# Two MLPs of a decoder trunk on one core: sweeps that begin with three plain pairs, chunks turned by half banks, and first conversions two pairs ahead

## The chip, the cores and the metric

The kernel runs on 1 core of one Trainium2 chip. The metric is the time of one execution on the device in microseconds (us), as the median of several runs. TensorE (PE in the profile, PEld for its weight loads) multiplies, ScalarE (ACT) and VectorE (DVE) convert, evacuate and normalise, SyncE (SP) issues the loads. All weights stream from HBM once.

## The reference

A trunk of two layers on 256 tokens of width 2048, in float32. Layer 0 mixes tokens by retention, layer 1 by block-sparse attention. Each layer then has an MLP and a gated per-layer embedding; every step begins with an RMS norm of the residual stream `h`.

```
def sq_relu_mlp(xn, w_up, w_down):
    return jnp.square(jax.nn.relu(xn @ w_up)) @ w_down

def per_layer_embed(h, p_i, g, w_up, w_gate):
    gate = jax.nn.sigmoid(rms_norm(h, g) @ w_gate)
    return (p_i @ w_up) * gate

for i in range(DEPTH):
    h = h + (retention or moba_attention)(rms_norm(h, ...))
    h = h + sq_relu_mlp(rms_norm(h, mlp_norm_g[i]), mlp_w_up[i], mlp_w_down[i])
    h = h + per_layer_embed(h, p[i], ple_norm_g[i], ple_w_up[i], ple_w_gate[i])
```

w_up is 2048 x 8192, w_down 8192 x 2048. The change concerns the product with w_down and what follows it.

## The kernel before

**High and low halves.** TensorE works on float32r. Every operand is split into a rounded high half and the remainder: `split` has ACT cast the high half and DVE subtract it from the source. A product is three matmuls (high by high, high by low, low by high). Weights arrive in raw pairs of 128 x 2048 float32, 1 MB, in `RAWS = 3` buffers; a load is issued on SP when an earlier raw buffer is free. The halves go to `wh` and `wl`, rings of `RING = 3` buffers each.

**Units.** The program is a list of units, each a run of matmuls on TensorE (as a rule on half a raw pair). Beside it stand two kinds of work with a due unit: conversions in the list `prep`, written ahead of the unit they are due at, and tasks (`at`), written behind theirs. `run` writes it all out in this order, and each engine executes its own instructions in the order written, so that an instruction that waits holds up all behind it on its engine.

**The MLP.** In `mlp` each layer goes through two halves of the 8192 columns. `phase_a` makes the activations of a half in 32 up tiles of 128 (two units each, names `up`). Each tile occupies one of four PSUM banks (tag `mm`) until `fold` has emptied it: ACT copies one half of the bank (L254), DVE adds the other (L255). Then DVE clamps and scales (L650), ACT squares (L651), and `split` makes the operand `a`. After that come two sweeps per half, so four per layer (sweeps 1 to 4; `dn00`, `dn01`, `dn10`, `dn11` in the program, `dn_` with a number in the trace). A sweep adds the product of all activations of the half with 1024 columns of w_down to two chunks of `h`, each 512 wide, for both groups t of 128 tokens.

**Plain and fast pairs.** A sweep (`sweep`) has 16 raw pairs of two units. A plain pair has 8 products, 4 per unit, into the four banks C00, C01, C10, C11 (first digit t, second the chunk): 24 matmuls. The pairs in `FAST` use a Strassen-like scheme with 7 products, 21 matmuls: 9 in the first unit, 12 in the second. For it DVE forms sums of the raw weights (`sums`, L605 to L607, `tsum`), `corner` converts three quarters of the raw pair for the first unit, and the sums are converted for the second (`wide`), which starts with the product into bank P5. `due` says ahead of which unit a pair's conversions are written: the first unit of the ring buffer before.

**The end of a sweep.** Behind the last fast pair, `rest` adds up the fast products in four tasks (`one` to `four`, L685 to L699), one after each of the next units. `done` adds the C banks to `h` on DVE (L672), for t = 0 behind the last unit but one, for t = 1 behind the last. The banks so emptied are those that the next sweep, or the embedding, takes. In the second half the sweep has then finished two chunks of `h`, and `finish` prepares them as operands of the next norm: `square` on ACT, then `turn`, eight transposes on TensorE into two banks (tag `aux`, two in all), and `split`, which calls `scaled` four times: each time ACT (L261) and then DVE (L262) reads half a bank, ACT and DVE taking turns. Sweep 4 is followed by the embedding (`ple`): four units `pu` of 12 matmuls into two banks of the tag `mm` each, which ACT copies out (L736), then the gate's units, which need the turned chunks.

Of the kernel before, what the change touches and what calls it, by code (L numbers as in the profile page):

```python
# [10 lines left out]
F32 = mybir.dt.float32  # L11
F32R = mybir.dt.float32r
I32 = mybir.dt.int32
AF = mybir.ActivationFunctionType
ALU = mybir.AluOpType
AX = mybir.AxisListType

P = 128
S = 256
# [18 lines left out]
WARM = 9  # L38
FILL = 5
BR = 32  # L40
FAST = (2, 4, 6, 9, 11, 13)
RAWS = 3
RING = 3
G_RET, G_MLP0, G_PLE0, G_KV, G_ATT, G_MLP1, G_PLE1, G_FIN = range(8)
# [36 lines left out]
class Core:  # L81
# [175 lines left out]
    def scaled(self, n, g, src):  # L257
# [4 lines left out]
        self.nc.vector.scalar_tensor_tensor(t[:, S:], src, gs, t[:, :S].bitcast(F32), op0=ALU.mult, op1=ALU.subtract)  # L262
        return t

    def square(self, c):

        if c == 0:
            self.ssq = self.cp.tile([P, 2, KD // 4], F32, name="ssq", tag="ssq", bufs=2)
        for t in range(2):
            self.nc.scalar.activation(self.slot("sq"), self.h[c][:, t], AF.Square, accum_out=self.ssq[:, t, c:c + 1])  # L270

    def finish(self, c, i, gains):

        self.square(c)
        st = {}

        def turn():
            for a in range(2):
                ps = st[a] = self.aux("xt")
                for b in range(2):  # L280
                    for t in range(2):
                        o, f = 2 * b + t, 2 * a + b
                        self.nc.tensor.transpose(ps[:, o * P:(o + 1) * P], self.h[c][:, t, f * P:(f + 1) * P], self.ident)

        def split(f, g, xs):
            n, b = 4 * c + f, f % 2
            xs[n] = self.scaled(n, g, st[f // 2][:, b * S:(b + 1) * S])
        self.at(i + 1, turn)
        for f in range(4):
            self.at(i + 1 + f // 2, lambda f=f: split(f, gains[0], self.xx))  # L290
            if len(gains) > 1:
                self.at(i + 3 + f, lambda f=f: split(f, gains[1], self.x2))
# [256 lines left out]
    def sweep(self, name, src, first, pairs, x, done, rest):  # L549

        banks, left = {}, {}
        tags = {"P1": "y", "P5": "y", "Q6": "aux", "Q7": "aux"}

        def add(s, ops):
            for bank, _, _ in ops:
                left[bank] = left.get(bank, 0) + 1

            def mm():
                h, l = (s[n].rearrange("p a (b c) -> p (a b) c", b=2) for n in "hl")
                m = self.nc.tensor.matmul  # L560
                for bank, which, j in ops:
                    start = bank not in banks
                    if start:
                        banks[bank] = self.bank(f"{name}{bank}_", *((tags[bank], 2) if bank in tags else ()))
                    left[bank] -= 1
                    ps, (xh, xl) = banks[bank], x(*which)
                    m(ps, xh, h[:, j], start=start, stop=False)
                    m(ps, xh, l[:, j], start=False, stop=False)
                    m(ps, xl, h[:, j], start=False, stop=left[bank] == 0)
            self.units.append(mm)  # L570
            return len(self.units) - 1
        for q in range(pairs):
            a, b, due = 2 * q, 2 * q + 1, self.slots[-1]["first"]
            s = self.begin(src, first + q)
            if q in FAST:
                last = q
                add(s, [("C01", (q, "S4"), 1), ("C00", (b, 0), 2), ("P1", (a, 0), 0)])
                t = {"first": len(self.units), "pair": s["pair"]}
                self.slots.append(t)
                e = add(t, [("P5", (q, "S1"), 0), ("Q6", (q, "S2"), 1), ("C10", (b, 1), 2), ("Q7", (q, "S3"), 3)])  # L580
                self.prep.append((due, lambda s=s, t=t: self.sums(s, t)))
                self.prep.append((due, lambda s=s: self.corner(s)))
                self.prep.append((s["first"], lambda t=t: self.wide(t, t["t"], 2 * UC)))
            else:
                for r in range(2):
                    i = add(s, [(f"C{r}{c}", (k, r), j) for c, ks in ((0, ((a, 0), (b, 2))), (1, ((a, 3), (b, 1)))) for k, j in ks])
                self.prep.append((due, lambda s=s: self.whole(s)))
        for n, fn in enumerate(rest(banks)):
            self.at(e + 1 + n, fn)
        self.at(i - 1, lambda: done(banks, 0, i))  # L590
        self.at(i, lambda: done(banks, 1, i))
# [17 lines left out]
    def mlp(self, layer, gains):  # L609
        nc = self.nc  # L610
        v = nc.vector
        st = {}
        b = len(self.units)
# [8 lines left out]
        def x(k, t):  # L622
# [5 lines left out]
            z = act[k]  # L628
            if k // 2 in FAST and k % 2 == 0:
                return z[:, 0], z[:, 1]  # L630
            return z[:, t * P:(t + 1) * P], z[:, S + t * P:S + (t + 1) * P]

        def combine(q):
            z = pair.pop(q).rearrange("p a (b c) -> p (a b) c", b=2)
            f = self.slot("sf", (P, 4, P))
            v.tensor_sub(f[:, 0:2], z[:, 0::3], z[:, 1:2].to_broadcast([P, 2, P]))
            v.tensor_add(f[:, 2], f[:, 1], z[:, 0])
            v.tensor_sub(f[:, 3], z[:, 2], f[:, 2])
            sums[q] = h, l = self.slot("sh", dt=F32R), self.slot("sl", dt=F32R)
            self.split(h, l, f.rearrange("p a b -> p (a b)"))  # L640
        for half in range(2):
            def evac_up(n, ps, half=half):
                q = n // 2
                if n % 2 == 0:
                    pair[q] = self.slot("t", (P, 2, S))
                t = pair[q][:, n % 2]
                self.fold(t, ps)
                for _ in range(4 if half == 0 and n < LEAD else 1):
                    yield
                v.scalar_tensor_tensor(t, t, 0.0, st["rb"], op0=ALU.max, op1=ALU.mult)  # L650
                nc.scalar.activation(t, t, AF.Square)  # L651
                if q in FAST and n % 2 == 0:
                    j = FAST.index(q)
                    if j % 2 == 0:
                        st["c"] = self.slot("ac", (P, 4, P), F32R)
                    act[n] = st["c"][:, 2 * (j % 2):2 * (j % 2) + 2]
                    self.split(act[n][:, 0], act[n][:, 1], t[:, :P])
                else:
                    act[n] = self.slot(f"a{n}", dt=F32R)
                    self.split(act[n][:, :S], act[n][:, S:], t)  # L660
                if n % 2:
                    if q not in FAST:
                        pair.pop(q)
                        return
                    yield
                    combine(q)
            self.phase_a(f"up{half}_", f"mlp_up{layer}", half * 64, 32, 2, 1 if half else LEAD, lambda k: self.xx[k], evac_up)

            def done(banks, t, i, g, half=half):
                for c in range(2):  # L670
                    h = self.h[2 * g + c][:, t]
                    v.tensor_add(h, h, banks[f"C{t}{c}"])  # L672
                if half and t:
                    for c in range(2):
                        self.finish(2 * g + c, i + 2 * c, gains)

            def rest(banks, g):
                z = {}

                def h(t, c):  # L680
                    return self.h[2 * g + c][:, t]

                def one():
                    z["q"], z["u"] = self.slot("q"), self.slot("u")
                    nc.scalar.copy(z["q"], banks["P1"])  # L685
                    v.tensor_add(h(0, 0), h(0, 0), z["q"])

                def two():
                    v.tensor_sub(z["q"], z["q"], banks["Q6"])
                    v.tensor_add(z["u"], z["q"], banks["P5"])  # L690
                    v.tensor_sub(h(0, 1), h(0, 1), z["u"])

                def three():
                    v.tensor_add(z["q"], z["q"], banks["Q7"])
                    v.tensor_add(h(1, 0), h(1, 0), z["q"])

                def four():
                    v.tensor_add(z["q"], z["q"], banks["P5"])
                    v.tensor_sub(h(1, 1), h(1, 1), z["q"])  # L699
                return [one, two, three, four]  # L700

            src, n = f"mlp_dn{layer}", FH // 256
            for g in range(2):
                self.sweep(f"dn{half}{g}_", src, (half * 2 + g) * n, n, x, lambda banks, t, i, g=g, done=done: done(banks, t, i, g),
                           lambda banks, g=g, rest=rest: rest(banks, g))
# [357 lines left out]
```

## Time and profile before

| | us |
|---|---|
| median of 3 runs (lowest, highest) | 2752.36 (2751.19, 2755.58) |
| the profiled execution, its own time | 2752.92 |
| its span, from the first instruction to the last | 2750.5 |
| TensorE busy, share of the span | 2722.4, 99% |
| DVE busy, ACT busy | 1924.7, 1406.5 |

The profile is of one execution. Its time is 2.42 us more than its span, and 0.56 us more than the median. Sweep 1 of layer 0 starts at 925.80 us of the span, sweep 2 at 1010.60, sweep 3 at 1271.69, sweep 4 at 1355.07 and the embedding behind it at 1446.75; in layer 1 sweep 1 starts at 2115.97, sweep 3 at 2462.09, sweep 4 at 2545.47, the embedding at 2637.25. In rows of the timeline the first number is the start in us and the second the time taken; brackets tell how long the engine was idle before it, and what released it. The granted clock is TensorE's, 1.00 being full speed.

### The profile page before, as it was taken

The numbers are of one execution on the slowest core, as the hardware profiler recorded it, in microseconds if no ns is written. First come the engines' busy times: TensorE is split into PE (matmuls) and PEld (weight loads), VectorE is DVE, ScalarE is ACT, GpSimd is POOL, SyncE is SP. The second block draws the span as 40 slices with busy tenths as digits, with TensorE's granted clock in tenths as the row PEclk, the third lists the DMA queues.
The fourth block names the chain that finished last, engine by engine and source line by source line (L and its number), as shares of the span: only waits on it lengthen the run. The fifth ranks groups of instructions, "written<-read, shape, count | busy, mean of one in ns | idle before, by whom it ended". The sixth has DMA issues, their size and how long they took to land.

```text
span 2750.5 us, 33950 instructions
## 1 busy us (share of the span) xinstructions
PE 2722.4 (99%) x13608; PEld 2310.3 (84%) x13608; DVE 1924.7 (70%) x2543; ACT 1406.5 (51%) x1926; POOL 0.2 (0%) x4
## 2 busy tenths in 40 slices
PE   9999999999999999999999999999999999999998
PEld 8888888888888888888787888888888888888786
DVE  7766666655566788667786677675676887668775
ACT  6444444444455545555555655554555445554554
POOL 0000000000000000000000000000000000000000
PEclk9999999999999999999999999999999999999999
DMA  7555555445555555555554555555455655545453
GB/s 285 185 187 186 187 187 181 180 181 199 183 178 199 188 199 214 184 199 184 184 211 176 180 188 176 176 184 184 168 200 179 215 191 198 197 175 213 171 209 138
DMA packets 79449, 522.48 MB, mean 190 GB/s; under 512 B 8987, under 2 KB 12988, under 8 KB 17596
## 3 DMA queue, kind: packets, MB, share of 16 engines
q1 hardware_dynamic: 78476, 519.20, 52.7%
q10 hardware_dynamic: 816, 1.11, 0.3%
q8 instruction: 107, 1.75, 0.3%
q14 instruction: 50, 0.41, 0.0%
HBM read 517.39 MB, written 2.88 MB: 189 GB/s over the span
## 4 chain that ended last, share of the span: by engine, by line
PE 81%; DVE 10%; ACT 7%; issue 2%; DMA 0%; ACTq 0%; SPq 0%; DVEq 0%
PE up L183 9%; DVE wl L250 6%; PE up L181 5%; ACT wh L249 4%; PE qk L183 4%; PE aq L183 2%; PE ak L183 2%; PE qk L181 2%; PE aq L181 1%; PE ak L181 1%; ACT t L651 1%; DVE t L650 1%; ACT a L249 1%; DVE t L255 1%; PE y L492 1%
## 5 line engine op out<-in xcount | busy, mean ns | idle before, releaser
L250 DVE TENSOR_TENSOR wl<-raw,wh 128x1024 fp32r<-128x1024 f32 (+3 forms) x843 | 1121.5, 1350 | 396.3 <-ACT wh L249 396.0
L249 ACT CAST wh<-raw 128x1024 fp32r<-128x1024 f32 (+3 forms) x843 | 952.3, 1151 | 370.3 <-issue 77.9
L183 PE MATMUL up<-x,wh 128*128 128x512 f32 x2048 | 490.5, 391 | 0.0
L183 PEld LDWEIGHTS up<-x,wh 128*128 128x128 f32 x2048 | 376.0, 188 | 72.5
L181 PEld LDWEIGHTS up<-x,wl 128*128 128x128 f32 x2048 | 263.3, 191 | 10.9 <-issue 0.6
L181 PE MATMUL up<-x,wl 128*128 128x256 f32 x2048 | 267.0, 283 | 0.0
L249 ACT CAST wh<-tsum 128x2048 fp32r<-128x2048 f32 x48 | 91.8, 1913 | 161.0 <-DVE tsum L607 129.0
L651 ACT ACTIVATE t<-t 128x256 f32<-128x256 f32 x128 | 53.5, 418 | 228.5 <-DVE t L650 228.5
L250 DVE TENSOR_TENSOR wl<-tsum,wh 128x2048 fp32r<-128x2048 f32 x48 | 110.0, 2292 | 29.1 <-ACT wh L249 29.1
L250 DVE TENSOR_TENSOR a<-t,a 128x256 fp32r<-128x256 f32 x104 | 44.3, 426 | 95.9 <-ACT a L249 95.9
L183 PE MATMUL qk<-x,wh 128*128 128x512 f32 x448 | 109.9, 392 | 0.0
L183 PEld LDWEIGHTS qk<-x,wh 128*128 128x128 f32 x448 | 81.8, 188 | 15.5
L261 ACT ACTIVATE x<-xt,g 128x256 fp32r<-128x256 f32 x112 | 52.1, 478 | 52.6 <-DVE x L262 43.4
L262 DVE SCALAR_TENSOR_TENSOR x<-xt,g,x 128x256 fp32r<-128x256 f32 x112 | 52.7, 482 | 27.4 <-ACT x L261 26.2
L254 ACT COPY t<-up 128x256 f32<-128x256 f32 x128 | 47.0, 367 | 44.9 <-PE up L183 44.8
L183 PE MATMUL aq<-x,wh 128*128 128x512 f32 x256 | 63.3, 391 | 0.0
L183 PE MATMUL ak<-x,wh 128*128 128x512 f32 x256 | 62.9, 391 | 0.0
L270 ACT ACTIVATE sq<-h 128x512 f32<-128x512 f32 x48 | 30.1, 627 | 62.0 <-DVE h L534 27.7
L181 PEld LDWEIGHTS qk<-x,wl 128*128 128x128 f32 x448 | 57.4, 191 | 2.2
L255 DVE TENSOR_TENSOR t<-t,up 128x256 f32<-128x256 f32 x128 | 53.2, 416 | 7.7 <-ACT t L254 7.4
L605 DVE TENSOR_TENSOR tsum<-raw 128x1024 f32<-128x1024 f32 x48 | 58.5, 1218 | 0.0
L181 PE MATMUL qk<-x,wl 128*128 128x256 f32 x448 | 58.1, 283 | 0.0
(1191 smaller groups left out, 5301.2 us busy)
## 6 DMA issues: line engine op xcount, KB each, us to landing
raw<-mlp_up SPq DMA_DIRECT2D x128, 1024.0 KB, 4.8
raw<-mlp_dn SPq DMA_DIRECT2D x128, 1024.0 KB, 4.8
raw<-ret_in SPq DMA_DIRECT2D x94, 1024.0 KB, 4.8
raw<-att SPq DMA_DIRECT2D x48, 1024.0 KB, 4.8
raw<-ret_out SPq DMA_DIRECT2D x32, 1024.0 KB, 4.8
raw<-ple_gate SPq DMA_DIRECT2D x32, 1024.0 KB, 4.8
raw<-att_o SPq DMA_DIRECT2D x16, 1024.0 KB, 4.8
raw<-ple_up SPq DMA_DIRECT2D x4, 1024.0 KB, 5.0
```

Source lines behind the costliest of these rows:

```text
L181: mm(ps[:, S:], wl[:, c], rhs[k][:, :S], start=False, stop=end)
L183: mm(ps, wh[:, c], rhs[k], start=first and k == 0, stop=end)
L249: self.nc.scalar.copy(dst_h, src)
L250: self.nc.vector.tensor_sub(dst_l, src, dst_h.bitcast(F32))
L254: self.nc.scalar.copy(dst, ps[:, :S])
L255: self.nc.vector.tensor_add(dst, dst, ps[:, S:])
L261: self.nc.scalar.activation(t[:, :S], src, AF.Copy, scale=gs)
L262: self.nc.vector.scalar_tensor_tensor(t[:, S:], src, gs, t[:, :S].bitcast(F32), op0=ALU.mult, op1=ALU.subtract)
L270: self.nc.scalar.activation(self.slot("sq"), self.h[c][:, t], AF.Square, accum_out=self.ssq[:, t, c:c + 1])
L492: mm(ys[t], a, w, start=i == 0, stop=i == len(ops) - 1)
L605: v.tensor_add(o[:, 0::3], r[:, 0:2], r[:, 3:4].to_broadcast([P, 2, 512]))
L651: nc.scalar.activation(t, t, AF.Square)
```

## The change

It has three parts.

1. `FAST` begins at pair 3 and takes every other pair from there; as many pairs as before are fast.
2. `due` of the first two pairs of a sweep lies one ring buffer further ahead: pair 0's conversions are written ahead of the last but three unit of the stage before, pair 1's ahead of the last but one. Before, they were written ahead of the last but one and ahead of the sweep's own first unit.
3. Behind sweeps 3 and 4, `drip` takes the place of `finish`. It turns half a chunk at a time, four transposes into one bank, behind units 1, 2, 4 and 5 of sweep 4, or behind units 2, 3, 5 and 7 of the embedding, and one unit later `scaled2` makes two operands: ACT twice, then DVE twice. `finish` stays for the other stages.

```
-FAST = (2, 4, 6, 9, 11, 13)
+FAST = (3, 5, 7, 9, 11, 13)
...
+    def scaled2(self, n, g, src):
+        out = []
+        for b in range(2):
+            t = self.slot(f"x{g}_{n + b}", dt=F32R)
+            out.append((t, src[:, b * S:(b + 1) * S], self.g[:, g, n + b:n + b + 1]))
+        for t, x, gs in out:
+            self.nc.scalar.activation(t[:, :S], x, AF.Copy, scale=gs)
+        for t, x, gs in out:
+            self.nc.vector.scalar_tensor_tensor(t[:, S:], x, gs, t[:, :S].bitcast(F32), op0=ALU.mult, op1=ALU.subtract)
+        return [t for t, _, _ in out]
...
+    def turn(self, c, a):
+        ps = self.aux("xt")
+        for b in range(2):
+            for t in range(2):
+                o, f = 2 * b + t, 2 * a + b
+                self.nc.tensor.transpose(ps[:, o * P:(o + 1) * P], self.h[c][:, t, f * P:(f + 1) * P], self.ident)
+        return ps
+
+    def drip(self, c, when, gain):
+        self.square(c)
+        for a, i in enumerate(when):
+            def first(a=a, i=i):
+                ps = self.turn(c, a)
+
+                def second():
+                    n = 4 * c + 2 * a
+                    self.xx[n], self.xx[n + 1] = self.scaled2(n, gain, ps)
+                self.at(i + 1, second)
+            self.at(i, first)
...
-            a, b, due = 2 * q, 2 * q + 1, self.slots[-1]["first"]
+            a, b, due = 2 * q, 2 * q + 1, self.slots[-2 if q < FAST[0] - 1 else -1]["first"]
...
-                    for c in range(2):
-                        self.finish(2 * g + c, i + 2 * c, gains)
+                    for c, when in enumerate(((2, 3), (5, 7)) if g else ((1, 2), (4, 5))):
+                        self.drip(2 * g + c, [i + k for k in when], gains[0])
```

What DVE has in its queue between sweeps 1 and 2 of layer 0, from `one` (the first row) to the addition that empties C00 (the last). `wl_7933` is the low half of pair 0 of sweep 2. Before:

```order
L686 TENSOR_TENSOR h0_89<-h0_89,q_7913 128x512
L689 TENSOR_TENSOR q_7913<-q_7913,dn00_Q6__7529 128x512
L690 TENSOR_TENSOR u_7914<-q_7913,dn00_P5__7525 128x512
L691 TENSOR_TENSOR h1_90<-h1_90,u_7914 128x512
L250 TENSOR_TENSOR wl_7933<-raw_7838,wh_7932 128x2048
L694 TENSOR_TENSOR q_7913<-q_7913,dn00_Q7__7536 128x512
L695 TENSOR_TENSOR h0_89<-h0_89,q_7913 128x512
L672 TENSOR_TENSOR h0_89<-h0_89,dn00_C00__7438 128x512
```

The same piece of DVE's queue after, with `wl_7902` for pair 0 and `wl_7939` for pair 1:

```order
L250 TENSOR_TENSOR wl_7902<-raw_7838,wh_7901 128x2048
L715 TENSOR_TENSOR h0_89<-h0_89,q_7919 128x512
L718 TENSOR_TENSOR q_7919<-q_7919,dn00_Q6__7559 128x512
L719 TENSOR_TENSOR u_7920<-q_7919,dn00_P5__7555 128x512
L720 TENSOR_TENSOR h1_90<-h1_90,u_7920 128x512
L250 TENSOR_TENSOR wl_7939<-raw_7881,wh_7938 128x2048
L723 TENSOR_TENSOR q_7919<-q_7919,dn00_Q7__7566 128x512
L724 TENSOR_TENSOR h0_89<-h0_89,q_7919 128x512
L701 TENSOR_TENSOR h0_89<-h0_89,dn00_C00__7438 128x512
```

Pair 0's subtraction went ahead of `one`, and pair 1's, which had stood behind all four additions of C banks, came in ahead of `three`. The queue between sweeps 3 and 4 reads alike.

ACT's queue between the up tiles and sweep 1 of layer 0, from the copy of up tile 29 to the copy of tile 31. `wh_7386` is the high half of pair 0. Before:

```order
L254 COPY t_7286<-up0_29_7301 128x256
L651 ACTIVATE t_7286<-t_7286 128x256
L249 CAST a29_7364<-t_7286 128x256
L254 COPY t_7383<-up0_30_7345 128x256
L249 CAST wh_7386<-raw_7220 128x2048
L651 ACTIVATE t_7383<-t_7383 128x256
L249 CAST a30_7411<-t_7383 128x256
L254 COPY t_7383<-up0_31_7392 128x256
```

After, where `wh_7345` belongs to pair 0 and `wh_7392` to pair 1:

```order
L254 COPY t_7286<-up0_29_7301 128x256
L249 CAST wh_7345<-raw_7220 128x2048
L680 ACTIVATE t_7286<-t_7286 128x256
L249 CAST a29_7370<-t_7286 128x256
L254 COPY t_7389<-up0_30_7351 128x256
L249 CAST wh_7392<-raw_7268 128x2048
L680 ACTIVATE t_7389<-t_7389 128x256
L249 CAST a30_7417<-t_7389 128x256
L254 COPY t_7389<-up0_31_7398 128x256
```

One wide cast stood between the copies of tiles 29 and 31, now two do.

ACT's queue in the embedding behind sweep 4 of layer 0; `x2_8` to `x2_11` are operands made of the first turned chunk. Before:

```order
L736 COPY pu0_0_11254<-pu0_0_11247 128x512
L736 COPY pu0_1_11263<-pu0_1_11256 128x512
L261 ACTIVATE x2_8_11275<-xt_11265,g_72 128x256
L261 ACTIVATE x2_9_11278<-xt_11265,g_72 128x256
L249 CAST wh_11243<-raw_11154 128x1024
L736 COPY pu1_0_11292<-pu1_0_11285 128x512
L736 COPY pu1_1_11301<-pu1_1_11294 128x512
L261 ACTIVATE x2_10_11303<-xt_11270,g_72 128x256
```

After:

```order
L765 COPY pu0_0_11254<-pu0_0_11247 128x512
L765 COPY pu0_1_11263<-pu0_1_11256 128x512
L249 CAST wh_11243<-raw_11154 128x1024
L765 COPY pu1_0_11276<-pu1_0_11269 128x512
L765 COPY pu1_1_11285<-pu1_1_11278 128x512
L249 CAST wh_11292<-raw_11178 128x1024
L765 COPY pu2_0_11303<-pu2_0_11296 128x512
L765 COPY pu2_1_11312<-pu2_1_11305 128x512
L272 ACTIVATE x2_8_11319<-xt_11287,g_72 128x256
```

The operands of the turned chunk moved behind the copies of the units `pu1` and `pu2`.

More of the change, by code (lines that the diff above doesn't have):

```diff
@@ L278, in turn @@
             for a in range(2):
[L279 to L283, printed above, removed]
+                st[a] = self.turn(c, a)
         def split(f, g, xs):
```

## The prediction

> **What bounds the kernel now.** I read the page first, then the waits of TensorE, then counts of matmuls in stretches of equal length, then the timeline around each place where a count was low.
>
> ```profile
> span 2750.5 us, 33950 instructions
> PE 2722.4 (99%) x13608; PEld 2310.3 (84%) x13608; DVE 1924.7 (70%) x2543; ACT 1406.5 (51%) x1926; POOL 0.2 (0%) x4
> ```
>
> TensorE has work nearly all the time, and the change neither adds nor removes a matmul. So it can only win back what TensorE loses to waits, and only lose by making new ones. The waits (engine, line, who was waited for: total, times, longest):
>
> ```profile
> PE xt L283 <- DVE x L262: 4.5, 2, 2.3
> PE dn_P__10774 L567 <- ACT wh L249: 2.0, 1, 2.0
> ```
>
> All sizeable ones lie at starts of down-projection sweeps (`dn`) or just behind the last sweep of a layer (`xt`). A wait is priced too low there, since a matmul's end is modelled; so I count matmuls in stretches instead. Columns: stretch, length, busy time and count of PE, PEld, DVE, ACT, POOL, granted clock, DMA share, GB/s.
>
> ```profile
> 980.00:1010.00 30.00, 30.00 (x134) 24.86 (x133) 26.90 (x24) 15.38 (x9) 0.00 (x0) 1.00 0.65 233
> 1010.60:1030.60 20.00, 20.00 (x90) 16.57 (x89) 16.29 (x14) 8.71 (x5) 0.00 (x0) 1.00 0.45 162
> 925.80:945.80 20.00, 19.27 (x82) 14.73 (x81) 16.33 (x17) 10.61 (x11) 0.00 (x0) 1.00 0.53 187
> 1271.69:1291.69 20.00, 19.87 (x88) 16.15 (x87) 16.68 (x15) 11.69 (x10) 0.00 (x0) 1.00 0.60 209
> 1355.07:1385.07 30.00, 25.73 (x111) 20.16 (x110) 22.09 (x22) 15.35 (x20) 0.00 (x0) 0.94 0.38 135
> 1446.75:1476.75 30.00, 27.51 (x122) 22.32 (x121) 20.04 (x38) 18.84 (x34) 0.00 (x0) 0.94 0.41 146
> 2115.97:2135.97 20.00, 19.05 (x81) 14.55 (x80) 16.33 (x17) 10.39 (x11) 0.00 (x0) 1.00 0.54 182
> 2462.09:2482.09 20.00, 19.88 (x88) 16.15 (x87) 16.68 (x15) 11.69 (x10) 0.00 (x0) 1.00 0.59 210
> 2545.47:2575.47 30.00, 25.73 (x111) 20.12 (x110) 22.09 (x22) 15.36 (x20) 0.00 (x0) 0.94 0.38 135
> 2637.25:2667.25 30.00, 27.74 (x131) 22.98 (x130) 21.67 (x42) 18.85 (x32) 0.00 (x0) 1.00 0.56 199
> 1375.10:1378.50 3.40, 3.22 (x8) 2.54 (x9) 3.40 (x3) 0.97 (x1) 0.00 (x0) 0.50 0.12 17
> 1457.01:1460.42 3.41, 1.27 (x8) 1.16 (x9) 2.30 (x4) 2.86 (x7) 0.00 (x0) 1.00 0.56 178
> 1460.43:1463.83 3.40, 3.40 (x10) 2.63 (x9) 2.29 (x4) 2.23 (x4) 0.00 (x0) 0.50 0.31 130
> 2566.35:2569.75 3.40, 3.40 (x10) 2.63 (x9) 3.33 (x4) 0.13 (x1) 0.00 (x0) 0.50 0.23 43
> 2644.85:2648.26 3.41, 2.07 (x12) 1.51 (x10) 2.19 (x3) 2.86 (x6) 0.00 (x0) 1.00 0.00 0
> 2648.27:2651.67 3.40, 2.49 (x13) 2.19 (x14) 2.19 (x3) 2.85 (x6) 0.00 (x0) 1.00 0.89 308
> ```
>
> The first two rows are clean: 134 matmuls in 30 us, 90 in 20 us, one per 0.227 us (30.00 us over 132 full starts). The next eight begin at sweep 1, sweep 3, sweep 4 and the embedding of layer 0, then the same of layer 1 (sweep 2 is the second clean row). The four 30 us stretches hold 16 transposes; eight of them take 0.79 us, the time of 3.5 matmuls:
>
> ```profile
> 1357.79 1.03 PE L283 MATMUL xt<-ident,h 128*128 128x128 f32 x8
> 1358.58 0.48 PE L567 MATMUL dn_C__10678<-wh,a 128*128 128x512 f32 x1
> ```
>
> so a clean one would hold 134 - 7 + 16 = 143. Missing are 8, 2, 32, 21 and 9, 2, 32, 12 matmuls: 118 x 0.227 = 26.8 us. Each count can be one too high, by where a stretch is cut, so I take 25.8 us as the most that can come back. Three stretches at clock 0.50 are inside it, each behind a wait of 2 us or more.
>
> **Sweep 4 (32 + 32 missing).** TensorE waits there for the sums of the first fast pair (dn_P above), whose cast stands behind the turned chunks' x on ACT:
>
> ```profile
> 1370.64 0.47 ACT L261 ACTIVATE x<-xt,g 128x256 fp32r<-128x256 f32 x1 [0.57 <-DVE x L262]
> 1371.02 1.89 ACT L249 CAST wh<-tsum 128x2048 fp32r<-128x2048 f32 x1
> ```
>
> After: the first fast pair is the fourth, units 7 and 8 of the sweep. The last work ahead of its cast is that of the fourth half bank, turned behind unit 5. From that turn to the second matmul on the sums, which needs DVE's half, TensorE has unit 6, nine matmuls of unit 7 and one of unit 8: 12 + 9 + 1 = 22, or 5.0 us. ACT needs 0.94 for two x and 1.89 for the cast, DVE 2.29 (as in 1004.41 below): 5.1 us. I take a wait of 0.1 us per sweep; ends 0 (all hidden) and 2.7 us (a unit of 12 later).
>
> **Sweeps 2 and 4: a new wait.** This is what the early conversions cost. DVE and ACT at the start of sweep 2:
>
> ```profile
> 999.91 1.91 ACT L249 CAST wh<-raw 128x2048 fp32r<-128x2048 f32 x1 [0.32 <-PE dn_Q__7536 L569]
> 1001.56 0.69 DVE L686 TENSOR_TENSOR h<-h,q 128x512 f32<-128x512 f32 x1
> 1004.41 2.29 DVE L250 TENSOR_TENSOR wl<-raw,wh 128x2048 fp32r<-128x2048 f32 x1
> 1006.61 0.68 DVE L694 TENSOR_TENSOR q<-q,dn_Q__7536 128x512 f32<-128x512 f32 x1
> 1007.93 0.68 DVE L672 TENSOR_TENSOR h<-h,dn_C__7438 128x512 f32<-128x512 f32 x1
> 1005.36 1.92 ACT L249 CAST wh<-raw 128x2048 fp32r<-128x2048 f32 x1 [3.53 <-PE dn_C__7464 L569]
> 1010.60 0.39 PE L567 MATMUL dn_C__7976<-wh,a 128*128 128x512 f32 x1
> ```
>
> 1004.41 is pair 0's subtraction, 1005.36 pair 1's cast, which waits for TensorE to free the third ring buffer, so it can't start earlier for being written earlier. Now pair 0's subtraction stands ahead of L686 (999.91 + 1.91, so 1001.84 to 1004.05), then come L686 to L691 (2.85, from 1001.56 to 1004.41) until 1006.90, and then pair 1's subtraction, ahead of L694. It waits for the cast, which ends at 1007.28, and holds DVE until 1009.51 (2.20 from 1004.41 to 1006.61). L694 follows, and 1.32 later the addition that empties bank C00: 1010.83 to 1011.51. The new sweep's first matmul needs that bank at 1010.60. It waits 0.9 to 1.0. Sweep 4 has the same queue order, and I charge both sweeps of both layers: 4 x 1.0 = 4.0 us. Ends: 0, if TensorE finds another bank, and 2.2 each, if pair 1's cast starts a whole 1.2 us later. The other three banks follow in the order in which they are needed, so I charge the first alone.
>
> **Sweep 1: the wait changes its place.** Here (8 and 9 missing) it was pair 0's low half that came late; moved two pairs ahead it doesn't. But ACT's queue now has two wide casts between the evacuations of up tiles 29 and 31:
>
> ```profile
> 918.94 0.36 ACT L254 COPY t<-up 128x256 f32<-128x256 f32 x1
> 920.66 0.42 DVE L650 SCALAR_TENSOR_TENSOR t<-t,rb 128x256 f32<-128x256 f32 x1
> 922.15 1.90 ACT L249 CAST wh<-raw 128x2048 fp32r<-128x2048 f32 x1
> 927.97 0.41 DVE L255 TENSOR_TENSOR t<-t,up 128x256 f32<-128x256 f32 x1
> 925.80 0.39 PE L567 MATMUL dn_C__7438<-wh,a 128*128 128x512 f32 x1
> 2109.34 0.37 ACT L254 COPY t<-up 128x256 f32<-128x256 f32 x1
> ```
>
> After tile 29's copy (919.3) comes the cast of pair 0 (1.90) and DVE's half (2.20), and only then L650 of tile 29: 923.4 for 920.66, 2.75 later. From there to tile 31's addition (927.97) the sequence is as before, with pair 1 in pair 0's place, so that addition ends at 928.38 + 2.75 = 931.13. It frees the bank that C11 takes, 18 matmuls into the sweep: 925.80 + 18 x 0.227 = 929.88. Wait 1.3 us; in layer 1, where tile 29's copy is 6.63 us ahead of the sweep (2115.97) instead of 6.86, 1.5 us. Sum 2.8 us, for 3.9 lost now; ends 0 and 2 x (1.5 + 1.7), the 1.7 being half of a stretch at clock 0.50. Sweep 3 has the same queue order, but only 2 + 2 matmuls missing; I take these to come back whole (worst: the 1.5 of sweep 1).
>
> **Behind sweep 4 (21 and 12 missing).** The second turn of eight waited 2.3 us for a bank that the x of the first turn held. Half banks, one turn after embedding unit 2, 3, 5 and 7, always find one free. What is late next:
>
> ```profile
> 1449.21 0.68 DVE L672 TENSOR_TENSOR h<-h,dn_C__10678 128x512 f32<-128x512 f32 x1
> 1452.72 1.05 ACT L736 COPY pu<-pu 128x512 f32<-128x512 f32 x2
> 2642.76 1.05 ACT L736 COPY pu<-pu 128x512 f32<-128x512 f32 x2
> ```
>
> Unit 2 is due 12 matmuls after 1446.75, at 1449.47, and its bank is freed at 1449.89: 0.45 with the hand-over. Unit 3 follows 2.72 and a turn of 0.4 later, at 1453.1, and needs the first half of 1452.72's copies: 0.2. In layer 1 the copies come 5.51 behind unit 1's start (2637.25), not 5.97: the first wait is gone, the second is 0.2 again. Sum 0.85; ends 0 and 2.4, the wait that went.
>
> **Costs I put at nothing.** x in pairs per half bank: as many instructions, one hand-over between ACT and DVE for three, off TensorE's path. Six fast pairs stay six, now every other one: the first clean row is such a stretch, DVE at 26.90 of 30 with no matmul lost. If that cover goes, DVE lacks 3.1 us in 30. Loads on SP keep their order and start when a conversion frees their buffer, earlier by this change; POOL has no part.
>
> **Sum.** 25.8 - (0.2 + 4.0 + 2.8 + 0.85) = 17.9 us saved of the profiled execution's 2752.92 us (span 2750.5): 2735.0. The median of the runs is 0.56 lower, so 2734.5.
>
> **A rule weighed.** The clock of a stretch of 3.4 us went to 0.50 where TensorE had been busy for 1.27 us of the stretch ahead of it (1457.01, then 1460.43), and stayed at 1.00 behind one with 2.07 (2644.85, then 2648.27). A new wait of 1.5 us leaves 3.41 - 1.5 + 0.16 = 2.07 (a matmul counts as busy for 0.39 where the next starts after 0.227), on the safe side by a hair. So I charge no clock. The Trainium skill (TensorE: Matmul & The Clock Gate, Part 1) has the clock halved only after an idle window of about 3.4 us. By that rule the waits of 2 us would have cost no clock, the three slow stretches (3 x 1.7 us) would not be among what comes back, and the time would be 2739.6; the trace disagrees, with clock 0.50 behind a stretch that was busy for 1.27 us.
>
> **Rivals.**
> - Everything comes back, 25.8 us: 2726.5. For it: DVE and ACT idle enough on average. Against: the two queues above are in order. Chance 0.12.
> - Sweep 4's wait moves to the fourth pair: the last half bank comes a unit later, 2.7 us and half a slow stretch, 1.7, twice: 8.8 back, 2743.3. For it: a margin of nothing between 5.0 and 5.1. Against: no other work of ACT stands there. Chance 0.12.
> - The new waits of sweep 1 reach the clock's point: 2 x 1.7, 2737.9. Chance 0.06.
> - Slower: at all eight sweep starts the early conversions hold the banks beyond 2.3 us (1.0 plus what a late load adds to pair 1's cast), so each loses 2.3 + 1.7 = 4.0: 32 + 1 against 25.8, 2759.6. It decides from 3.1 us per start. For it: such waits did halve the clock. Against: pair 1's cast waited for TensorE, not for its load (1005.36), and sweep 3 hardly waits today. Chance 0.02.
> - The change does nothing, 2752.4: ring buffers, not queue order, set when conversions run. True of pair 1 in sweep 2, but sweep 4's fast pair does move. Chance 0.02.
>
> **How the numbers follow.** The forecast holds 0.66, by its own bounds 2730 to 2740; with most of the two larger rivals the range is 2727 to 2743. A measurement here can tell 0.2%, 5.5 us: faster 0.95, same 0.03, slower 0.02.
>
> **What the profile after would show.** Right: no clock of 0.50 but at the ends; no wait of `xt` or P5; new waits of about 1 us for the addition into h at the first matmul of sweeps 2 and 4, and of 1.3 to 1.5 us for L255's counterpart at C11 in sweep 1. Wrong: a wait at the fourth pair's sums in sweep 4, a slow stretch behind sweep 1, or banks free in time at sweeps 2 and 4.

## The result: 14.9 us faster, and the profile after

| | before | after |
|---|---|---|
| median of 4 runs each (lowest, highest), us | 2751.87 (2751.19, 2755.58) | 2737.01 (2736.33, 2737.74) |
| the profiled execution, its own time | 2752.92 | 2737.74 |
| its span | 2750.5 | 2735.8 |

The ratio is 0.9943, 95% interval 0.9926 to 0.9961. Of all the executions below, one of e5 took 4558.18 us at a granted clock of 0.555 where the other nine took 2749.40 to 2752.97, and e5's ratio is of those nine, its median of all ten. The forecast was 2734.5 with a range of 2727 to 2743: 2.5 us too low. As many matmuls run as before; the first lines of the page after:

```profile
span 2735.8 us, 33960 instructions
PE 2715.2 (99%) x13608; PEld 2307.2 (84%) x13608; DVE 1923.7 (70%) x2543; ACT 1406.5 (51%) x1926; POOL 0.2 (0%) x4
```

TensorE's waits in the down-projections and the embedding, after (engine, tile, line, who was waited for: total, times, longest):

```profile
PE dn_C__7464 L596 <- DVE t L255: 2.0, 1, 2.0
PE dn_C__17151 L596 <- DVE t L255: 1.4, 1, 1.4
PE dn_C__20335 L596 <- DVE h L701: 0.9, 1, 0.9
PE dn_C__7976 L596 <- DVE h L701: 0.9, 1, 0.9
PE dn_C__17663 L596 <- DVE h L701: 0.9, 1, 0.9
PE dn_C__10648 L596 <- DVE h L701: 0.9, 1, 0.9
PE pu L763 <- DVE h L701: 0.2, 1, 0.2
```

The waits of `xt` and of the sums are gone. Two new kinds stand there. The first matmul of sweeps 2 and 4 of both layers waits for the addition that empties C00 (7976, 10648, 17663, 20335), and sweep 1 of both layers waits at C11 for the addition of up tile 31 (7464, 17151). Counts of matmuls in stretches from the start of sweep 1 (20 us), sweep 4 and the embedding (30 us) of layer 0, then the same of layer 1; the last row is the 3.4 us around sweep 1's wait in layer 0:

```profile
925.80:945.80 20.00, 18.03 (x80) 14.58 (x79) 13.53 (x14) 9.97 (x11) 0.00 (x0) 1.00 0.56 207
...
1357.37:1387.37 30.00, 29.98 (x138) 24.44 (x139) 23.70 (x25) 16.81 (x23) 0.00 (x0) 1.00 0.41 149
1442.74:1472.74 30.00, 29.80 (x139) 24.23 (x138) 21.07 (x38) 18.63 (x34) 0.00 (x0) 1.00 0.51 182
2108.17:2128.17 20.00, 18.61 (x82) 15.12 (x81) 13.00 (x12) 10.02 (x10) 0.00 (x0) 1.00 0.55 198
...
2539.13:2569.13 30.00, 29.99 (x138) 24.45 (x139) 23.71 (x25) 16.80 (x23) 0.00 (x0) 1.00 0.42 149
2624.48:2654.48 30.00, 30.00 (x140) 24.45 (x139) 22.15 (x42) 18.85 (x33) 0.00 (x0) 1.00 0.60 211
930.35:933.76 3.41, 1.75 (x8) 1.43 (x9) 1.60 (x4) 2.34 (x6) 0.00 (x0) 1.00 0.76 271
```

Sweep 4 holds 138 matmuls where it held 111, the embedding 139 and 140 where it held 122 and 131; sweep 1 holds 80 and 82, no better than the 82 and 81 of before. The clock is 1.00 in each. From the first matmul of one stage to that of the next, sweep 4 became 6.31 and 6.44 us shorter, the stretch behind it 3.79 and 1.95; sweep 1 with the wait at sweep 2's start became 1.53 and 0.68 longer, sweep 3 with that at sweep 4's start 0.65 each.

Where the wait for C00 comes from, as the timeline after has it between sweeps 1 and 2 of layer 0:

```profile
1005.83 1.92 ACT L249 CAST wh<-raw 128x2048 fp32r<-128x2048 f32 x1 [3.04 <-PE dn_C__7464 L598]
...
1002.34 2.29 DVE L250 TENSOR_TENSOR wl<-raw,wh 128x2048 fp32r<-128x2048 f32 x1 [0.22 <-ACT wh L249]
...
1007.78 2.29 DVE L250 TENSOR_TENSOR wl<-raw,wh 128x2048 fp32r<-128x2048 f32 x1 [0.38 <-ACT wh L249]
1009.99 0.68 DVE L723 TENSOR_TENSOR q<-q,dn_Q__7566 128x512 f32<-128x512 f32 x1
...
1011.31 0.68 DVE L701 TENSOR_TENSOR h<-h,dn_C__7438 128x512 f32<-128x512 f32 x1
```

Pair 0's subtraction (1002.34) is done early. Pair 1's cast waits for TensorE (3.04), its subtraction on DVE (1007.78) waits for the cast, and `three` (L723) and the addition into h (L701) stand behind it. The wait at sweep 1's C11, same view:

```profile
919.81 0.36 ACT L254 COPY t<-up 128x256 f32<-128x256 f32 x1
...
931.54 0.41 DVE L255 TENSOR_TENSOR t<-t,up 128x256 f32<-128x256 f32 x1
...
932.01 0.50 PE L596 MATMUL dn_C__7464<-wh,a 128*128 128x512 f32 x1 [1.97 <-DVE t L255]
```

The time of the whole was forecast almost right. The experiments show that one of its reasons was not: a piece of the change that I priced at nothing brings most of the gain by itself.

### The profile page after: what moved, and what is told of

Same layout as the page of the kernel before. It is cut to its first block, busy times and chain, and to the rows that moved or that the text cites. A ratio compares the mean times of both kernels' runs of the same rounds, so it can differ in the third digit from the quotient of the medians.

```text
span 2735.8 us, 33960 instructions
## 1 busy us (share of the span) xinstructions
PE 2715.2 (99%) x13608; PEld 2307.2 (84%) x13608; DVE 1923.7 (70%) x2543; ACT 1406.5 (51%) x1926; POOL 0.2 (0%) x4
## 3 DMA queue, kind: packets, MB, share of 16 engines
q8 instruction: 107, 1.75, 0.2%
## 4 chain that ended last, share of the span: by engine, by line
PE 85%; DVE 7%; ACT 5%; issue 1%; DMA 1%; SPq 0%; ACTq 0%
PE up L183 10%; PE up L181 5%; DVE wl L250 4%; PE qk L183 4%; ACT wh L249 3%; PE aq L183 2%; PE ak L183 2%; PE qk L181 2%; PE aq L181 1%; PE ak L181 1%; ACT t L680 1%; DVE t L679 1%; PE pu L763 1%; ACT a L249 1%; DVE t L255 1%
## 5 line engine op out<-in xcount | busy, mean ns | idle before, releaser
L261 ACT ACTIVATE x<-xt,g 128x256 fp32r<-128x256 f32 x80 | 37.3, 480 | 35.1 <-DVE x L262 25.0
L183 PEld LDWEIGHTS ak<-x,wh 128*128 128x128 f32 x256 | 46.7, 188 | 8.7
```

The source lines that it names most:

```text
L183: mm(ps, wh[:, c], rhs[k], start=first and k == 0, stop=end)
L261: self.nc.scalar.activation(t[:, :S], src, AF.Copy, scale=gs)
```

## Experiments

Theory: each part has its own price. The early conversions make the six new waits and only cost; the places of the fast pairs and the half banks bring the gain. Rivals: the early conversions are a part of the gain; the places alone, or the half banks alone, would do. The table has the medians, the ratio to the runs of before beside them (2751.6 to 2752.1 each time) with its interval, and from each profile three lengths in us, layer 0 / layer 1: from sweep 1's first matmul to sweep 2's, from sweep 4's to the embedding's, and from the embedding's to sweep 1 of layer 1 / to the last matmul.

| kernel | median | ratio | sweep 1 | sweep 4 | behind it |
|---|---|---|---|---|---|
| before | 2751.87 | | 84.80 / 85.03 | 91.68 / 91.79 | 669.22 / 102.33 |
| after | 2737.01 | 0.9943 (0.9926 to 0.9961) | 86.33 / 85.71 | 85.37 / 85.35 | 665.43 / 100.38 |
| e1 after, nothing early | 2732.02 | 0.9921 (0.9906 to 0.9936) | 83.99 / 84.25 | 85.45 / 85.43 | 665.70 / 100.40 |
| e2 after, pair 0 alone early | 2730.68 | 0.9915 (0.9901 to 0.9930) | 83.76 / 83.47 | 85.71 / 85.71 | 665.61 / 100.39 |
| e3 before, places alone | 2742.83 | 0.9961 (0.9947 to 0.9975) | 84.34 / 84.09 | 87.40 / 87.41 | 669.27 / 103.93 |
| e4 before, `drip` alone | 2736.92 | 0.9939 (0.9924 to 0.9954) | 84.83 / 85.07 | 86.71 / 86.72 | 665.45 / 100.38 |
| e5 before, early alone | 2750.09 | 0.9995 (0.9985 to 1.0004) | 85.39 / 85.65 | 89.91 / 89.84 | 667.16 / 102.34 |
| e6 after, pair 1 alone early | 2736.23 | 0.9944 (0.9929 to 0.9958) | 85.02 / 85.29 | 85.35 / 85.38 | 665.37 / 100.43 |
| e7 after, old places | 2739.95 | 0.9956 (0.9941 to 0.9971) | 85.35 / 85.66 | 86.59 / 86.61 | 665.38 / 100.36 |
| e8 e2, operands in turns | 2737.26 | 0.9946 (0.9929 to 0.9962) | 83.33 / 83.23 | 90.19 / 88.57 | 665.78 / 100.38 |
| e9 before, operands grouped | 2738.48 | 0.9950 (0.9936 to 0.9963) | 84.80 / 85.05 | 86.23 / 86.27 | 666.49 / 101.40 |
| e10 e2, chunks turned whole | 2732.01 | 0.9926 (0.9911 to 0.9942) | 83.02 / 83.23 | 85.34 / 85.34 | 666.34 / 101.40 |
| e11 pair 0 early in sweep 1 | 2730.39 | 0.9920 (0.9907 to 0.9934) | 83.02 / 83.27 | 85.41 / 85.41 | 665.40 / 100.38 |
| e12 e2 again | 2730.60 | 0.9921 (0.9909 to 0.9934) | 83.19 / 83.25 | 85.67 / 85.69 | 665.45 / 100.39 |

**e1: after, with nothing early.**

```
-            a, b, due = 2 * q, 2 * q + 1, self.slots[-2 if q < FAST[0] - 1 else -1]["first"]
+            a, b, due = 2 * q, 2 * q + 1, self.slots[-1]["first"]
```

> After, but with both first pairs of a sweep due where they were before. Theory (queue order): the additions that empty C00 no longer stand behind pair 1's subtraction, so the four waits at the first matmul of sweeps 2 and 4 (1.07 each, 1.15 with the refill) go; sweep 1 loses to pair 0's low half again, 1.8 and 2.0 as before, in place of 2.25 and 1.66 for C11. Sweep 4 and the embedding keep what they won. 2737.0 - 4.6 - 0.1 = 2732.3. Rival (the early conversions bring the gain): sweep starts become slower and sweep 4 loses pair 1's low half; 2740 or more, up to 2752.

2732.02. No wait for C00 and none for C11 is left in its trace; sweep 1's second matmul waits for pair 0's low half (0.67 and 0.93 us more than its spacing). DVE's queue ahead of sweep 2:

```profile
1003.25 2.28 DVE L250 TENSOR_TENSOR wl<-raw,wh 128x2048 fp32r<-128x2048 f32 x1
...
1005.45 0.68 DVE L723 TENSOR_TENSOR q<-q,dn_Q__7566 128x512 f32<-128x512 f32 x1
...
1006.78 0.68 DVE L701 TENSOR_TENSOR h<-h,dn_C__7438 128x512 f32<-128x512 f32 x1
```

The subtraction between the additions is pair 0's here, which starts at 1003.25, and not pair 1's, which started at 1007.78. So C00 is empty at 1007.46, 2 us ahead of the sweep's first matmul (1009.44). So here the early conversions cost 5.0 us.

**e2 and e6: which of the two pairs.** e2 makes pair 0 alone early, e6 pair 1 alone.

```
e2:  self.slots[-2 if q < 1 else -1]["first"]
e6:  self.slots[-2 if q == 1 else -1]["first"]
```

> After, but with pair 0 alone due early, pair 1 as before. Theory (pair 1's subtraction ahead of the fast products' additions, and a second wide cast between the copies of up tiles 29 and 31, are what costs): no C00 wait in sweeps 2 and 4 (4.6 us back) and no C11 wait in sweep 1; there pair 1's low half is late instead, by 1.4 us in layer 0 and 0.6 in layer 1. 2737.0 - 4.6 - (2.25 + 1.66 - 1.4 - 0.6) = 2730.5. Rival (pair 0's own conversion, a wide one ahead of the evacuations, delays the banks): C00 and C11 waits stay, 2736 to 2737. Rival (both have to be early): pair 1 is late in all sweeps, about 1.5 in each of eight, 2742.

> After, with pair 1 alone due early and pair 0 where it was. Theory (what holds the banks is pair 1's subtraction ahead of the third addition of fast products, since it waits for a cast that waits for TensorE): the four C00 waits are there as in the changed kernel, 4 x 1.15; in sweep 1 pair 0's low half is late again and C11 waits about 0.9 in layer 0: 2732.0 + 4.6 + 0.5 = 2737. Rival (either pair's early place would do it, or only both): no C00 waits, 2732.

e2: 2730.68, with none of the six waits; the largest left are 0.64 us for pair 1's low half in sweep 1 of layer 0, 0.47 at the embedding of layer 0 and 0.43 for a low half in each sweep 4. e6: 2736.23, with the four C00 waits at 1.07 us each and 0.23 at C11. So pair 1's place makes the waits at C00: against after, moving it back gains 6.3 us. Pair 0 early is worth 1.3 (2732.02 to 2730.68, where the runs of e2 alone spread over 1.5); by the table it gains in sweep 1 and loses 0.26 and 0.28 in sweep 4.

**e3 and e4: the places alone, the half banks alone.** e3 is the kernel before with the first line of the diff:

```
-FAST = (2, 4, 6, 9, 11, 13)
+FAST = (3, 5, 7, 9, 11, 13)
```

e4 is after with that line and `due` put back, so before with `drip`, `turn` and `scaled2` alone.

> Before, with the new places of the fast pairs alone. Theory (the parts add up): the wait for the sums in sweep 4 goes with its slow stretch, 7.2 us in each layer; the embedding keeps its 21 and 12 missing matmuls and no C00 wait appears: 2751.9 - 14.4 = 2737.5. Rival (the half banks free ACT for the fast pair's cast): only a part of sweep 4's loss goes, 2745 to 2750.

> Before, with the turning by half banks alone. Theory (the parts add up): the embedding wins 3.8 + 1.95 = 5.75 us; in sweep 4 the cast of the first fast pair, still pair 2, now stands ahead of the second chunk's x but behind the first's, so half of its 14.4 us comes back: 2739. Ends 2746 (none of it) and 2732 (all). Rival (the places of the fast pairs alone matter): 2751.

The expectation of e3 missed, and e4 came out 2.1 below its 2739, inside its ends. The places alone bring 9.3 us, not 14.4: sweep 4 keeps waits at the fourth pair, and the embedding all of its own. TensorE's waits of e3:

```profile
PE xt L283 <- DVE x L262: 4.5, 2, 2.3
PE dn_C__10655 L568 <- DVE wl L250: 1.3, 1, 1.3
PE dn_C__20342 L568 <- DVE wl L250: 1.3, 1, 1.3
```

`drip` alone brings 15.2, as much as the whole change, with the first fast pair still at pair 2. One wait of 1.48 us is left in each of its sweeps 4, for a bank (tag `aux`) that a fast product takes and from which DVE is still making operands x; with the new places beside it (e1) it is gone:

```profile
PE dn_Q__10779 L596 <- DVE x L274: 1.3, 1, 1.3
```

The gains overlap: both take away the stretch at clock 0.50 in sweep 4, and both together, e1, bring 20.1 and not 24.5.

**e5 and e7: early alone, and all but the places.** In both, `due` has the constant 2 for `FAST[0] - 1`, so that the same two pairs are early.

> Before, with the conversions of the first two pairs two pairs ahead and nothing else. Theory (the early conversions only cost): four C00 waits of 1.15 each with the refill, sweep 1 losing 1.3 + 1.5 for C11 in place of 1.8 + 2.0, sweep 3 winning 2 x 0.45: 2751.9 + 4.6 - 1.0 - 0.9 = 2754.6. In sweep 4 the new wait at C00 may come off the wait for the sums behind it, 1 us in each layer: 2752.6. Rival (the early conversions are a part of the gain): 2740 to 2748.

> After, with the fast pairs at their old places. Theory (half banks and places both cure sweep 4's wait, so the places alone are worth what they were worth beside the half banks without early conversions, 2736.9 - 2732.0 = 4.9, less what the C00 wait of sweep 4 takes off the wait for x behind it, up to 2 x 1.07): 2737.0 + 4.9 - 2.1 = 2739.8. Ends 2737.7 and 2742. Rival (the places of the fast pairs carry sweep 4's gain): 2751.

e7 came out as expected, 2739.95: beside the rest of the change the places are worth 2.9 us. e5 was expected at 2752.6 to 2754.6 and gave 2750.09, no difference that can be measured. Its trace has the C00 waits (1.07 to 1.32) and the C11 waits (1.23 and 1.46). The wait at C00 of sweep 4 comes off the wait for the sums, as expected. The embedding of layer 0, whose text is that of before, became 2.06 us shorter (669.22 to 667.16): its wait of 2.41 fell so that the clock stayed at 1.00 (last section). That is not a gain of the edit.

**e8: the order of the operands.** Here I tested a price of nothing. In e2, a half bank's two operands are made in turns, as before:

```
-                    self.xx[n], self.xx[n + 1] = self.scaled2(n, gain, ps)
+                    self.xx[n], self.xx[n + 1] = [self.scaled(n + b, gain, ps[:, b * S:(b + 1) * S]) for b in range(2)]
```

> The version with pair 0 alone early (2730.7), but a half bank's two operands are made one after the other (ACT, DVE, ACT, DVE) in place of ACT twice and DVE twice. Theory (the order of the four is worth nothing, since it is off TensorE's path): 2730.7, within 1. Rival (the hand-overs between ACT and DVE hold the half banks and the cast behind them): waits for xt or for the sums of sweep 4 grow, 2732 to 2735.

2737.26: 6.6 us lost, more than either expectation; some 1.6 of it is one stretch at clock 0.50 in layer 0 (sweep 4 takes 90.19 there and 88.57 in layer 1). TensorE's waits in sweep 4 of e8:

```profile
PE dn_P__10804 L597 <- DVE wl L250: 1.8, 1, 1.8
PE dn_P__20491 L597 <- DVE wl L250: 1.8, 1, 1.8
PE dn_P__10804 L596 <- ACT wh L249: 0.8, 1, 0.8
PE dn_P__20491 L596 <- ACT wh L249: 0.8, 1, 0.8
```

These are the waits of before, for the first fast pair's cast and then its low half, though the pair is now the fourth. The timeline of e8 around them, ACT and then DVE:

```profile
1370.92 0.84 ACT L261 ACTIVATE x<-xt,g 128x256 fp32r<-128x256 f32 x2 [3.45 <-DVE x L262]
...
1372.71 1.89 ACT L249 CAST wh<-tsum 128x2048 fp32r<-128x2048 f32 x1
...
1368.74 1.75 DVE L250 TENSOR_TENSOR wl<-raw,wh 128x1536 fp32r<-128x1536 f32 x1
1370.41 0.48 DVE L262 SCALAR_TENSOR_TENSOR x<-xt,g,x 128x256 fp32r<-128x256 f32 x1
...
1374.63 2.29 DVE L250 TENSOR_TENSOR wl<-tsum,wh 128x2048 fp32r<-128x2048 f32 x1 [1.30 <-ACT wh L249]
```

ACT idles for 3.45 us ahead of the second operand of a half bank, until DVE has done the first (1370.41). DVE comes to that only after the fast pair's sums and the 1.75 of its first conversion. ACT's cast of the sums stands behind. The same row in the trace of before:

```profile
1369.22 0.84 ACT L261 ACTIVATE x<-xt,g 128x256 fp32r<-128x256 f32 x2 [3.46 <-DVE x L262]
```

The wait is in the program: two operands of one bank as ACT has them, in turns (before) and grouped (after):

```
L261 ACTIVATE x2_4_10730<-xt_10720,g_72 128x256 [waits PE_49]
L261 ACTIVATE x2_5_10733<-xt_10720,g_72 128x256 [waits DVE_49]

L272 ACTIVATE x2_4_10760<-xt_10728,g_72 128x256 [waits PE_49]
L272 ACTIVATE x2_5_10761<-xt_10728,g_72 128x256
```

ACT's second read of the bank waits for DVE's first read of it. The Trainium skill (PSUM — Partial Sum Buffer, "PSUM bank collisions raise a hardware error") says that two engines may not touch the same bank and quadrant at once, two reads included, so that software has to put them in order. What a program without that order would do is shown by no run here; what the order costs is.

**e9: that order alone, in the kernel before.** Eight transposes at once, old places, nothing early; only the operands behind sweeps 3 and 4 are grouped (the sweep passes `two=True`; `both` calls `scaled2` for a bank):

```
-            self.at(i + 1 + f // 2, lambda f=f: split(f, gains[0], self.xx))
+            if not two:
+                self.at(i + 1 + f // 2, lambda f=f: split(f, gains[0], self.xx))
+            elif f % 2 == 0:
+                self.at(i + 1 + f // 2, lambda f=f: both(f // 2))
```

> Before, with one thing changed: behind sweeps 3 and 4 two operands of a turned chunk are made by ACT twice and then DVE twice, instead of ACT, DVE, ACT, DVE. Eight transposes are still done at once, the fast pairs and the conversions stay. Theory (ACT's second operand waits 3.46 us for DVE, which is busy with the sums, and the fast pair's cast stands behind it): the wait for that cast in sweep 4 (2.16 + 0.61) goes, the wait for DVE's half of it stays at about 2.4, and the clock is not halved there: 4.9 + 3.4 back, and 0.6 per layer at the embedding: 2751.9 - 9.5 = 2742. Ends 2746 (clock still halved) and 2739. Rival (what counts is half a chunk at a time, not this order): 2751 to 2752.

2738.48, better than expected: 13.4 us from the order in which two engines take up a bank, against 14.9 for the whole change. Some 5 of the 13.4 are the three stretches at clock 0.50 of before, 1.7 each, which are gone with the waits. Timeline of e9:

```profile
1365.70 1.57 ACT L272 ACTIVATE x<-xt,g 128x256 fp32r<-128x256 f32 x4 [2.82 <-PE xt L295]
1367.14 1.93 ACT L249 CAST wh<-tsum 128x2048 fp32r<-128x2048 f32 x1
...
1368.12 1.66 DVE L274 SCALAR_TENSOR_TENSOR x<-xt,g,x 128x256 fp32r<-128x256 f32 x4
1369.69 2.28 DVE L250 TENSOR_TENSOR wl<-tsum,wh 128x2048 fp32r<-128x2048 f32 x1
```

ACT makes all four operands of the chunk in a row and is at the cast at 1367.14, where it came at 1371.02 before. In sweep 4 a wait of 1.08 for the low half is left, and at the embedding 1.48 where it was 2.45; the clock stays at 1.00 throughout.

**e10: chunks turned whole, operands grouped.** e2, with `drip` exchanged for e9's `finish`.

> The version with pair 0 alone early (2730.7), with chunks turned whole again, eight transposes at once, but with ACT twice and DVE twice. Theory (in sweep 4 the order of the operands is what helps; at the embedding it is the half banks, since the second chunk's transposes wait for a bank held behind the copies of pu): sweep 4 within 0.5 of the version it is made from; the embedding loses about 2 us of wait per layer, and 1.7 more where it halves the clock: 2730.7 + 4 = 2734.7, or 2738 with the clock. Rival (half banks are worth nothing beside the order): 2731.

2732.01. Sweep 4 is as short as in any kernel (85.34); the embedding waits 1.53 and 1.50 for `xt`, of which behind sweep 4 about 0.7 and 1.0 us of length remain, and it did not halve the clock. So half banks are worth 1.4 us beside the grouped order, which I had credited with the whole of the embedding's gain.

**e11 and e12: the best version.** e11 makes pair 0 early in sweep 1 alone (`self.slots[-2 if q < 1 and name == "dn00_" else -1]`), beside e2 once more.

> After, with pair 0 early in sweep 1 alone, and nothing early elsewhere. Theory (place by place): sweep 1 as in the version with pair 0 early everywhere (83.76 and 83.47 us from its start to sweep 2's), sweep 4 as with nothing early (85.45 and 85.43): 2730.7 - 0.5 = 2730.2. Rival (noise decides at this size): 2730 to 2732.

> The version with pair 0 alone early once more, beside the last one: 2730.7, within 0.5.

2730.39 and 2730.60: no difference between the two. Both beat before by 21 us and after by some 6.

## Why the prediction was right, and where it was wrong

**What could come back (25.8).** After's span is 14.7 us shorter, and its own waits with the refill of about 0.1 us behind each come to 9.9: together 24.6. So the bound was 1.2 too high. The clean count for 30 us with 16 transposes was the step: I took 143, and stretches with hardly a wait hold 138 to 140.

**Sweeps 2 and 4 (4 x 1.0).** Right in mechanism, place and size: 1.06 or 1.07 each, 4.6 with the refill. e6 and e2 show pair 1's subtraction to be the cause.

**Sweep 1 (1.3 + 1.5).** Right in mechanism; the term of layer 0 was mis-sized: 2.13 and 1.55 us, 3.9 with what followed. The chain from tile 29's copy to tile 31's addition was as worked out (11.73 us from 919.81 to 931.54, against 930.72 - 918.94 = 11.78). But I left tile 29's copy where it stood, and with the new places it came 0.87 later. Worked out from each trace, that copy starts in layer 0 4.4 to 4.5 us behind the start of its tile's last matmul in the five runs with the old places, and 4.6 to 5.4 in the nine with the new ones. So part 1 seems to move the up phase ahead of the sweep too, which I had not looked at. How much of the 0.87 is the change's is open: e2 and e12, the same kernel, have 5.3 and 4.8.

One reading behind this term was wrong: I put the 8 and 9 missing matmuls of before down to pair 0's low half. In that trace pair 0's low half comes late by 0.40 us in layer 0 and 0.63 in layer 1, about 0.1 more with the refill. Another 0.33 and 0.48 in each layer, 1.0 with the refill, are waits for low halves at the first fast pair (dn_C__7445 and dn_P__7525 in layer 0):

```profile
PE dn_P__7525 L568 <- DVE wl L250: 0.3, 1, 0.3
PE dn_C__7438 L568 <- DVE wl L250: 0.2, 1, 0.2
PE dn_C__7445 L568 <- DVE wl L250: 0.2, 1, 0.2
```

These two are gone where the new places stand and nothing is early (e1), and still there with `drip` alone (e4): it is the places that take them away.

**Behind sweep 4 (0.45 + 0.2, and 0.2).** Right in sum: 0.56 in layer 0, 0.29 in layer 1. The wait for unit 2's bank came (0.37 and 0.08 of refill in layer 0). Of the two waits of 0.2 for ACT's copies nothing clear is left: 0.11 us are lost at that place in each layer, where about 0.09 are lost behind every turn.

**Sweep 4's sums (0.1 each).** 0.18 and 0.17, with the refill 0.29: right in size, wrong in its reason. "After: the first fast pair is the fourth" names what the shift does, but the places alone left 1.50 + 0.48 there (e3), and with the fourth pair first but the operands in turns 0.99 + 2.10 (e8). My sum of 5.0 against 5.1 held because it had ACT make two x in a row (0.94), which is `scaled2`'s doing.

**"Costs I put at nothing."** This step failed. "As many instructions, one hand-over between ACT and DVE for three, off TensorE's path": the work that I named as off the path holds ACT for 3.45 us, and the cast on which TensorE waits is behind it. Its price is 6.6 us in e8 and 13.4 in e9. The row that says so was in the trace of before (1369.22, idle 3.46, released by DVE x); I had read the cast's place behind the x, and not what the x waited for.

**The clock.** "A new wait of 1.5 us" was taken to be on the safe side by a hair. Layer 1's wait of 1.55 came out so. Layer 0's was 2.13, left a stretch busy for 1.75, and the clock stayed at 1.00. That was luck in part: TensorE stood still from 930.04 to 932.01, and the stretch began at 930.35. Whole inside one stretch, the wait would have left 1.44 us of work, and no run here shows what follows that.

**The rivals.** Everything back: no kernel here came to 2726.5; the best ends at 2730.4. The wait at the fourth pair is real without the grouped order (e8: 6.6, against 8.8 worked out). The sweep 1 waits did not reach the clock's point. Slower from the early conversions: they cost 5.0 us (e1), 1.07 at each of four starts, far from the 3.1 from which it decides.

## What to carry to other kernels

Where two engines read one PSUM bank, let the first do all of its reads before the second begins: in turns, each in-order queue waits for the other's backlog, and what stands behind pays (13.4 us here, of which some 5 are the slower clock behind the waits). An instruction written early is early for its whole queue: before moving a conversion ahead, look at what it will wait for and what it then holds. And a part priced at nothing wants its own run.

## What the runs showed of the hardware

In the trace of before the three stretches at clock 0.50 last 3.413 us each. They begin at 1375.10, 1460.43 and 2566.35, so 85.33 and 1105.92 us apart, which is 25 and 324 such stretches. I read from this that TensorE's clock is set on a grid of stretches of 3.413 us, and the rows below show that what counts is how long TensorE was busy in the stretch before. e8 has the same two waits in both layers, and the clock was halved in one only. Stretches of e8, layer 0 and then layer 1 (length, busy time of PE with its count, PEld, DVE, ACT, POOL, clock, DMA share, GB/s):

```profile
1374.19:1377.60 3.41, 1.13 (x4) 0.73 (x5) 2.97 (x2) 3.41 (x3) 0.00 (x0) 1.00 0.13 55
1377.61:1381.01 3.40, 3.40 (x10) 2.66 (x9) 3.34 (x3) 0.16 (x1) 0.00 (x0) 0.50 0.27 43
2558.61:2562.02 3.41, 1.78 (x8) 1.48 (x9) 3.41 (x2) 2.42 (x2) 0.00 (x0) 1.00 0.00 0
2562.03:2565.43 3.40, 3.40 (x17) 2.81 (x16) 3.33 (x5) 0.35 (x1) 0.00 (x0) 1.00 0.58 188
```

In layer 1 the waits lay across the border of two stretches. In e5 at sweep 4 and at the embedding:

```profile
1371.39:1374.80 3.41, 0.61 (x2) 0.19 (x1) 2.24 (x2) 3.41 (x3) 0.00 (x0) 1.00 0.34 142
1374.82:1378.21 3.39, 3.30 (x8) 2.66 (x9) 3.37 (x3) 0.88 (x1) 0.00 (x0) 0.50 0.09 19
2644.56:2647.97 3.41, 1.75 (x10) 1.57 (x11) 2.29 (x4) 2.75 (x5) 0.00 (x0) 1.00 0.69 252
2647.98:2651.38 3.40, 3.40 (x17) 2.81 (x16) 2.28 (x4) 2.76 (x5) 0.00 (x0) 1.00 0.13 53
```

Over the traces here each stretch busy for 0.50 to 1.27 us was followed by clock 0.50, and none that was busy for 1.75 or more; nothing between was seen. The Trainium skill (TensorE: Matmul & The Clock Gate, Part 1) has the window at 3413 ns and free-running, which these rows bear out, and the half clock after an idle window, which they do not: 1.13 us of work was not enough to keep the clock. A wait of 2 to 3 us so costs its own length or 1.7 us more, by where the grid cuts it. Where two kernels differ by one such stretch, as before and e5 do at the embedding of layer 0, the 1.7 us need not come from their code.
